# Weight splits and layer 0's state space tables on GpSimd in a two-layer hybrid decoder step

## The chip, the cores and the metric

The kernel runs on one core of one Trainium2 chip. The metric is the device time of one execution in microseconds, as the median of several runs.

## What is computed

One inference step of a decoder trunk with two layers, for one prompt of 512 tokens and eight samples of 4 tokens each (544 columns together), model width 1024, all in float32. Each layer, cut to what matters:

```
mod  = silu(c) @ w_ada + b_ada                  # 6 x 1024 values for each sequence
h    = rms_norm(x) * (1 + scale1) + shift1
proj = h @ w_in                                 # 1024 -> 1536: q, k, v, u, xr, yg
o    = concat(norm(window_attention(q, k, v)),  # 8 heads, 2 kv heads, window 128
              norm(s5_mixer(u)),                # 16 groups, complex state of 64
              norm(rglru_mixer(xr, yg)))        # depthwise conv, gated recurrence
x    = x + gate1 * (o @ w_o)
h2   = rms_norm(x) * (1 + scale2) + shift2
x    = x + gate2 * conv_ffn(h2)                 # 1024 -> 5632 -> conv 3 -> gelu gate -> 1024
```

The outputs are x and the new caches and states. The s5 mixer is a diagonal complex recurrence; its step a_bar = exp(lambda dt) and the factors in front of B come from the parameters alone, so that their powers and products can be put into tables before the tokens are there.

## The kernel before

**Matrix products.** Tokens lie along the free axis, in two halves of 256 and 288 columns. Each float32 product is made of three fp32r products: the weight is split into a rounded high part and a low part, `lo = raw - hi`, the activations likewise into `hh` and `hl`, and `mm3` (L430) adds hi x hh, hi x hl and lo x hh in PSUM. A weight tile (128 x 8 x 128) takes 48 such matmuls for both halves.

**Weights.** `Weights.ahead` (L407 to L417) loads the next weight of a fixed order into one of three `raw` buffers (L412, on the DMA queue of SyncE, SP), ScalarE rounds it to `whi` (L415), VectorE subtracts `wlo = raw - whi` (L416). There are six pairs of `whi` and `wlo`. Each time a weight has been used up, `done` frees its pair and calls `ahead` for one more. So the next six weights are split ahead of use. The `raw` buffers are shared with the slabs of the modulation weights `wada` (L507), of 512 KB each, which TensorE multiplies directly (L524); a `raw` buffer is free again when its slab has been multiplied, or its weight been split.

**Stages.** A start (the first slabs, the first norm, three weights), then for each layer the mixers and the feed-forward. In the mixers 12 column blocks of `w_in` are multiplied one after the other; each one's result starts a chain (attention, state space, recurrence) written as a generator, and after each product `tick` lets every chain take a step, lets attention do a unit, and lets the background do one slab of modulation weights. The 8 blocks of `w_o` follow as soon as all parts of `o` are there. In the feed-forward 44 blocks of `w_up` and three passes of 8 blocks of `w_down` follow each other, and layer 1's tables are made in the background. Tile, the framework, takes the order of the calls as priorities and settles each engine's order when the program is built; on the chip each engine and each DMA queue works its list strictly in order.

**Tables of the state space part.** `ssm_rot` (L759) makes the rotations `er`, `ei` for both halves of the groups in four stages, each by a complex product `cmul` (L577): four products, a difference, a sum. `ssm_tables` (L682) makes, for each half h, three complex products of 64, 192 and 256 elements per partition, widens them on ScalarE, multiplies them on TensorE into a direct kernel `kk`, clears a tile (L741), and spreads `kk` over it through a scratch tensor in DRAM (L744, L746). All tables are written to DRAM by DMAs on GpSimd's queue (`emit_tab`, L670) and read back on SP's queue (`load_tabs`, L678) by `ssm_chain`. In layer 0 this is called at the start of the mixers, between the first group of products, and the second half's tables go on as one of the chains. The tiles come from an arena of free tiles; `ssm_chain` waits for eight of them, so it follows the tables of the other half.

**GpSimd** does nothing else now than clear the `kz` tiles (L1459) and start DMAs: the tables above and the outputs.

Of the kernel before, what the change touches and what calls it, by code (L numbers as in the profile page):

```python
# [316 lines left out]
def trunk(ctx: ExitStack, tc: tile.TileContext, A, O):  # L317
    nc = tc.nc
    V, S, T_, G = nc.vector, nc.scalar, nc.tensor, nc.gpsimd
# [6 lines left out]
    def const(name, shape, dt=F32, pool=cp):  # L326
        return pool.tile(list(shape), dt, name=name)
# [59 lines left out]
    def f32(ap):  # L387
        return ap.bitcast(F32)
# [8 lines left out]
    class Weights:  # L397


        def __init__(self, order):  # L400
            self.order = list(order)
            self.free = [(const(f"whi{i}", (128, 8, 128), F32R), const(f"wlo{i}", (128, 8, 128), F32R))
                         for i in range(NW)]
            self.at = {}
            self.slot = {}

        def ahead(self, n=NW):  # L407
            while self.order and self.free and n:
                n -= 1
                key, src, kt = self.order.pop(0)  # L410
                raw = wp.tile([128, 8, 128], F32, tag="raw", name="raw", bufs=NRAW)[:, :kt]
                nc.sync.dma_start(raw, src)  # L412
                self.slot[key] = self.free.pop(0)
                hi, lo = (z[:, :kt] for z in self.slot[key])
                S.copy(hi, raw)  # L415
                V.tensor_sub(lo, raw, f32(hi))  # L416
                self.at[key] = (hi, lo)  # L417

        def __getitem__(self, key):
# [154 lines left out]
        ts(ki, k, 127.0, 8388608.0, OP.add, OP.mult)  # L574
        stt(out, pl, 1.0, ki.bitcast(F32), OP.add, OP.mult)

    def cmul(ore, oim, ar, ai, br, bi, t):  # L577
        V.tensor_mul(t, ai, bi)
        V.tensor_mul(ore, ar, br)
        V.tensor_sub(ore, ore, t)  # L580
        V.tensor_mul(t, ai, br)
        V.tensor_mul(oim, ar, bi)
        V.tensor_add(oim, oim, t)

    def ssm_params(l):
        d = LY[l]
# [77 lines left out]
    def bc(ap, w):  # L664
        return ap[:, :, None].to_broadcast([128, 4, w])
# [16 lines left out]
    def ssm_tables(l, h):  # L682
        d = LY[l]
        pw, kap = d["pw"], d["kap"]
        q = slice(4 * h, 4 * h + 4)
        yield from slots(7)
        raw, tm_, Z = R(512), R(512), R(512)
        nc.sync.dma_start(raw[:, 0:256].rearrange("p (a b) -> p a b", a=4),
                          A["ssmw"][l, :, :, q, :].rearrange("p a j c -> p a (j c)"))
        nc.sync.dma_start(raw[:, 256:512].rearrange("p (a b) -> p a b", a=2),  # L690
                          A["ssmc"][l, :, :, q, :].rearrange("p a j c -> p a (j c)"))
        rw = raw[:, 0:256].rearrange("p (a j c) -> p a j c", a=4, j=4)
        c0r = raw[:, 256:384].rearrange("p (j c) -> p j c", j=4)
        tm = tm_[:, 0:256].rearrange("p (j a c) -> p j a c", j=4, a=4)
        C0i = tm_[:, 256:384].rearrange("p (j c) -> p j c", j=4)
        Zr, Zi = (Z[:, 256 * i:256 * i + 256].rearrange("p (j s c) -> p j s c", j=4, s=4) for i in range(2))

        def bcn(ap, n):
            return ap[:, q, :, None].to_broadcast([128, 4, n, 16])

        def many(ap, n):
            return ap[:, :, None, :].to_broadcast([128, 4, n, 16])

        def widen(z, sign):

            o = R(512)
            ov = o.rearrange("p (j s g c) -> p j s g c", j=4, s=4, g=2)
            for g in range(2):
                act(ov[:, :, :, g], z, AF.Copy, scale=gm[:, sign + g:sign + g + 1])
            return o  # L710

        yield 1
        cmul(Zr[:, :, 3], Zi[:, :, 3], bc(kap[0][:, q], 16), bc(kap[1][:, q], 16), rw[:, 0], rw[:, 1], tm[:, :, 0])
        cmul(Zr[:, :, 0:3], Zi[:, :, 0:3], bcn(d["pwd"][0], 3), bcn(d["pwd"][1], 3),
             many(Zr[:, :, 3], 3), many(Zi[:, :, 3], 3), tm[:, :, 0:3])
        Br, Bi = widen(Zr, 0), widen(Zi, 0)
        Brv, Biv = (z.rearrange("p (j s c) -> p j s c", j=4, s=4) for z in (Br, Bi))
        yield 1
        ts(C0i, raw[:, 384:512].rearrange("p (j c) -> p j c", j=4), -1.0)
        cmul(Zr, Zi, bcn(d["pwu"][0], 4), bcn(d["pwu"][1], 4), many(rw[:, 2], 4), many(rw[:, 3], 4), tm)  # L720
        Cr, Ci = widen(Zr, 0), widen(Zi, 2)
        Crv, Civ = (z.rearrange("p (j d c) -> p j d c", j=4, d=4) for z in (Cr, Ci))
        yield 1
        pk = one()
        for part, (bb, c0, cc) in enumerate(((Brv, c0r, Crv), (Biv, C0i, Civ))):
            for jj in range(4):
                rows = slice(32 * jj, 32 * jj + 32)
                T_.matmul(pk[rows, 0:32], bb[:, jj, 3, :], c0[:, jj, :], start=part == 0, stop=part == 1,
                          skip_group_check=True)
            for jj in range(4):  # L730
                rows = slice(32 * jj, 32 * jj + 32)
                T_.matmul(pk[rows, 32:128], bb[:, jj, 3, :],
                          cc[:, jj, 0:3].rearrange("p d c -> p (d c)"), start=False, stop=part == 1,
                          skip_group_check=True)
        kk = sp.tile([128, 128], F32, tag="kk", name="kk", bufs=1)
        S.copy(kk, pk[:, :128])
        PS.put(pk)
        dg = d["prm"]("ssmd")[:, 32 * h:32 * h + 32]
        V.tensor_add(kk[:, 0:32], kk[:, 0:32], dg)
        tz = Z  # L740
        V.memset(tz, 0.0)  # L741
        tzv = tz.rearrange("p (j t) -> p j t", j=4)
        scr = tc.dram_tile([4, 32, 128], F32, name=f"kscr{l}{h}")
        G.dma_start(scr.rearrange("j c t -> (j c) t"), kk)  # L744
        for s in range(4):
            G.dma_start(tzv[32 * s:32 * s + 32, :, 32 * s:128],  # L746
                        scr[:, :, 0:128 - 32 * s].rearrange("j c t -> c j t"))
        emit_tab(l, h, "tz", tz)
        emit_tab(l, h, "cr", Cr)
        emit_tab(l, h, "ci", Ci)  # L750
        for n, z, o in (("br", Br, raw), ("bi", Bi, tm_)):
            yield 1
            ps = one()
            for jj in range(4):
                T_.transpose(ps[:, jj * 128:jj * 128 + 128], z[:, jj * 128:jj * 128 + 128], eye)
            S.copy(o, ps)
            PS.put(ps)
            free(z)
            emit_tab(l, h, n, o)  # L759
        d["ready", h] = True  # L760

    def ssm_rot(l):
        d = LY[l]
        E = []
        for h in range(2):
            er, ei = T(512), T(512)
            er, ei = (z.rearrange("p (j k) -> p j k", j=4) for z in (er, ei))
            V.memset(er[:, :, 0:1], 1.0)
            V.memset(ei[:, :, 0:1], 0.0)
            E.append((er, ei))  # L770
        tm = T(512)
        for st in range(4):
            m, n = (1, 1) if st == 0 else (2 * 4 ** (st - 1), 3)
            for h in range(2):
                er, ei = E[h]
                q = slice(4 * h, 4 * h + 4)

                def grid(z, lo, k):
                    return z[:, :, lo:lo + k * m].rearrange("p j (r k) -> p j r k", k=m)

                def factor(i):
                    return d["pow3"][i][:, st, q, 0:n, None].to_broadcast([128, 4, n, m])

                def base(z):
                    return z[:, :, None, 0:m].to_broadcast([128, 4, n, m])

                tv = tm[:, :4 * n * m].rearrange("p (j r k) -> p j r k", j=4, r=n)
                cmul(grid(er, m, n), grid(ei, m, n), factor(0), factor(1), base(er), base(ei), tv)
            yield
        free(tm)  # L790
        for h in range(2):
            emit_tab(l, h, "er", E[h][0].rearrange("p j k -> p (j k)"))
            emit_tab(l, h, "ei", E[h][1].rearrange("p j k -> p (j k)"))
# [942 lines left out]
    free(sg_)  # L1736
    W_ = Weights(weights_order())
    for l in range(L):
        with tc.tile_pool(name=f"mix{l}", bufs=1, reuse_waits="tile") as pool, ExitStack() as stack:
            banks(f"mb{l}", stack, 0, 4)  # L1740
            assert AR.kept == 0
# [43 lines left out]
            mixers(l, pool)  # L1785
            AR.free = [t for t in AR.free if any(t is p for p in perm)]
            assert len(AR.free) == NF, len(AR.free)
        with tc.tile_pool(name=f"ffn{l}", bufs=1, reuse_waits="tile") as pool, ExitStack() as stack:
            banks(f"fb{l}", stack, 1, 2)
            if l + 1 < L:  # L1790
                bg.append(tables(l + 1))
            ffn(l, pool)
            flush()
# [18 lines left out]
```

## Time and profile before

| what | value |
|---|---|
| median of 3 runs | 1328.41 us (1324.43 to 1328.97) |
| profiled execution | 1335.0 us |
| its span, first to last instruction | 1333.2 us |
| TensorE busy | 1270.1 us, 95% |
| VectorE busy | 881.8 us, 66% |
| ScalarE busy | 576.5 us, 43% |
| GpSimd busy | 48.8 us, 4% |

Busy times are those of engine instructions; waiting, branching and the issuing of DMAs on SP's and ScalarE's queues do not count here, while GpSimd's own DMA instructions do. PE is TensorE, PEld its weight loads, DVE VectorE, ACT ScalarE, POOL GpSimd. A time in the rows is counted from the first instruction of the span. Layer 0's mixers run from the start to about 295 us, layer 1's from about 700 to 930 us; the feed-forward parts lie behind each.

### The profile page before, as it was taken

How to read it: one execution, taken by the hardware profiler on the slowest of the kernel's cores; microseconds unless marked ns; L12 is line 12 of the kernel's file. 1: busy time of each engine (PE TensorE's matmuls, PEld its weight loads, DVE VectorE, ACT ScalarE, POOL GpSimd, SP SyncE). 2: the span in 40 equal slices, each digit the busy share in tenths (PEclk: the TensorE clock that was granted, in tenths of full speed). 3: DMA queues.
4: the chain of work that ended last, by engine and by line, in shares of the span. 5: the costliest groups of instructions: out<-in, count | busy, mean ns of one | idle time of the engine just before them, and what ended most of it. 6: DMA issues, size and time to landing. Idle time of an engine off the chain costs nothing.

```text
span 1333.2 us, 26368 instructions
## 1 busy us (share of the span) xinstructions
PE 1270.1 (95%) x10438; PEld 1164.8 (87%) x10438; DVE 881.8 (66%) x2583; ACT 576.5 (43%) x1112; POOL 48.8 (4%) x82
## 2 busy tenths in 40 slices
PE   4899988999999999999999999899999999999998
PEld 2666765799999999999998776679999999999998
DVE  8787885988774556456576877668865456545651
ACT  4557544356542343234354466545643234313430
POOL 0021010000020000000000001000000000000000
PEclk9899999999999999999999999999999999999999
DMA  8876677533343223334235846602322332233221
GB/s 294 279 265 215 191 252 229 178 111 118 93 135 125 85 86 87 97 93 115 76 108 180 268 142 203 191 14 90 110 81 86 96 95 74 86 97 94 85 72 51
DMA packets 72460, 178.24 MB, mean 134 GB/s; under 512 B 15584, under 2 KB 26752, under 8 KB 72336
## 3 DMA queue, kind: packets, MB, share of 16 engines
q1 hardware_dynamic: 65456, 162.08, 39.1%
q0 software_dynamic: 4960, 11.68, 2.5%
q10 hardware_dynamic: 1920, 2.79, 0.7%
q8 instruction: 82, 1.34, 0.4%
q14 instruction: 42, 0.34, 0.1%
HBM read 159.37 MB, written 14.34 MB: 130 GB/s over the span
## 4 chain that ended last, share of the span: by engine, by line
PE 83%; DMA 9%; DVE 5%; ACT 2%; issue 1%; POOL 0%; SPq 0%; DVEq 0%; POOLq 0%; ACTq 0%
PE wide L430 42%; PE fb1w L430 9%; PE fb0w L430 8%; DMA raw<-in_wada_dram 6%; PE fb0s L430 5%; PE fb1s L430 4%; PE mb0s L430 3%; PE mb1s L430 3%; PE mb0s L524 1%; PE mb1s L524 1%; DMA raw<-in_wo_dram 1%; DVE wlo L416 1%; DMA f<-in_ssmh_dram 1%; DMA tab_br<-f 1%; PE mb1s L1242 0%
## 5 line engine op out<-in xcount | busy, mean ns | idle before, releaser
L430 PE MATMUL wide<-hh,whi 128*128 128x288 f32 (+1 forms) x1360 | 400.3, 295 | 1.2 <-ACT hh L897 0.8
L430 PE MATMUL wide<-hl,whi 128*128 128x288 f32 (+1 forms) x1360 | 395.9, 291 | 0.0
L430 PE MATMUL wide<-hh,wlo 128*128 128x288 f32 (+1 forms) x1360 | 394.3, 290 | 0.0
L416 DVE TENSOR_TENSOR wlo<-raw,whi 128x1024 fp32r<-128x1024 f32 (+1 forms) x176 | 211.0, 1200 | 187.1 <-ACT whi L415 183.1
L415 ACT CAST whi<-raw 128x1024 fp32r<-128x1024 f32 (+1 forms) x176 | 180.4, 1029 | 274.8 <-PE wide L430 125.8
L430 PEld LDWEIGHTS wide<-hh,whi 128*128 128x128 f32 x1360 | 257.2, 189 | 18.3 <-issue 14.0
L430 PEld LDWEIGHTS wide<-hl,whi 128*128 128x128 f32 x1360 | 257.1, 189 | 6.3 <-issue 6.1
L430 PEld LDWEIGHTS wide<-hh,wlo 128*128 128x128 f32 x1360 | 259.2, 191 | 3.0 <-issue 3.0
L380 DVE SCALAR_TENSOR_TENSOR f<-wide,prm,f 128x511 f32<-128x511 f32 x236 | 100.2, 485 | 0.0
L430 PE MATMUL wide<-mid,whi 128*128 128x256 f32 (+1 forms) x526 | 99.8, 287 | 0.0
L430 PEld LDWEIGHTS wide<-mid,whi 128*128 128x128 f32 x526 | 82.4, 188 | 0.0
L897 ACT CAST mid<-f 128x544 fp32r<-128x544 f32 x44 | 28.5, 647 | 122.4 <-DVE f L1660 119.1
L430 PE MATMUL wide<-mid,wlo 128*128 128x256 f32 (+1 forms) x263 | 75.5, 287 | 0.0
L377 ACT ACTIVATE f<-f 128x544 f32<-128x544 f32 x50 | 33.0, 659 | 89.2 <-DVE f L1650 84.5
L430 PE MATMUL fb1w<-hh,whi 128*128 128x256 f32 (+1 forms) x240 | 69.4, 289 | 1.8 <-ACT hh L862 1.3
L430 PE MATMUL fb1w<-hl,whi 128*128 128x256 f32 (+1 forms) x240 | 69.4, 289 | 0.0
L430 PE MATMUL fb1w<-hh,wlo 128*128 128x256 f32 (+1 forms) x240 | 68.8, 287 | 0.0
L430 PE MATMUL fb0w<-hh,whi 128*128 128x256 f32 (+1 forms) x224 | 64.7, 289 | 1.6 <-ACT hh L862 1.1
L430 PE MATMUL fb0w<-hl,whi 128*128 128x256 f32 (+1 forms) x224 | 64.7, 289 | 0.0
L430 PE MATMUL fb0w<-hh,wlo 128*128 128x256 f32 (+1 forms) x224 | 64.3, 287 | 0.0
L430 PE MATMUL fb0s<-mid,whi 128*128 128x288 f32 (+1 forms) x326 | 62.9, 290 | 0.0
L430 PE MATMUL fb1s<-mid,whi 128*128 128x288 f32 (+1 forms) x308 | 59.1, 289 | 0.0
(612 smaller groups left out, 2542.2 us busy)
## 6 DMA issues: line engine op xcount, KB each, us to landing
raw<-in_wada_dram SPq DMA_DIRECT2D x92, 512.0 KB, 5.2
raw<-in_wup_dram SPq DMA_DIRECT2D x88, 512.0 KB, 3.5
raw<-in_wdn_dram SPq DMA_DIRECT2D x32, 448.0 KB, 3.3
raw<-in_win_dram SPq DMA_DIRECT2D x24, 512.0 KB, 4.2
raw<-in_wo_dram SPq DMA_DIRECT2D x16, 512.0 KB, 4.5
raw<-in_wdn_dram SPq DMA_DIRECT2D x16, 512.0 KB, 3.5
e<-q ACTq DMA_DIRECT2D x32, 68.0 KB, 4.6
out_ox_dram<-x SPq DMA_DIRECT2D x8, 272.0 KB, 2.1
```

Source lines behind the costliest of these rows:

```text
L377: return S.activation(out, in_, f, bias=bias, scale=scale, **kw)
L380: return V.scalar_tensor_tensor(out, a, s, b, op0=op0, op1=op1, **kw)
L415: S.copy(hi, raw)
L416: V.tensor_sub(lo, raw, f32(hi))
L430: T_.matmul(out, w[wi][:, k, :], r[ri][:, a:b], start=first and i == 0, stop=last and i == 2)
L524: T_.matmul(ps[32 * g:32 * g + 32], silu[:, k, :], have[n][:, g], start=k == 0, stop=k == 7, skip_group_check=True)
L897: S.copy(dst[0], src)
```

## The change

In `Weights` the engine of the subtraction becomes a variable, which is GpSimd at the start and in the mixers, and VectorE in the feed-forward. `cmul` takes an engine; in `ssm_tables` and `ssm_rot` this is GpSimd for layer 0 and VectorE for layer 1, and so is the engine that clears the tile before the direct kernel is spread. The memsets at the start of `ssm_rot` and the sign change `C0i` stay on VectorE.

```
@@ Weights
+            self.low = G
...
                 S.copy(hi, raw)
-                V.tensor_sub(lo, raw, f32(hi))
+                self.low.tensor_sub(lo, raw, f32(hi))
@@ cmul
-    def cmul(ore, oim, ar, ai, br, bi, t):
-        V.tensor_mul(t, ai, bi)
-        V.tensor_mul(ore, ar, br)
-        V.tensor_sub(ore, ore, t)
-        V.tensor_mul(t, ai, br)
-        V.tensor_mul(oim, ar, bi)
-        V.tensor_add(oim, oim, t)
+    def cmul(ore, oim, ar, ai, br, bi, t, eng=None):
+        z = eng or V
+        z.tensor_mul(t, ai, bi)
+        z.tensor_mul(ore, ar, br)
+        z.tensor_sub(ore, ore, t)
+        z.tensor_mul(t, ai, br)
+        z.tensor_mul(oim, ar, bi)
+        z.tensor_add(oim, oim, t)
@@ ssm_tables
+        eng = V if l else G
...
-             many(Zr[:, :, 3], 3), many(Zi[:, :, 3], 3), tm[:, :, 0:3])
+             many(Zr[:, :, 3], 3), many(Zi[:, :, 3], 3), tm[:, :, 0:3], eng)
...
-        V.memset(tz, 0.0)
+        eng.memset(tz, 0.0)
@@ ssm_rot
-                cmul(grid(er, m, n), grid(ei, m, n), factor(0), factor(1), base(er), base(ei), tv)
+                cmul(grid(er, m, n), grid(ei, m, n), factor(0), factor(1), base(er), base(ei), tv, V if l else G)
@@ main loop
     for l in range(L):
+        W_.low = G
...
             mixers(l, pool)
...
+        W_.low = V
         with tc.tile_pool(name=f"ffn{l}", bufs=1, reuse_waits="tile") as pool, ExitStack() as stack:
```

The other two calls of `cmul` in `ssm_tables` take `eng` in the same way.

## Rows read from the trace of the kernel before

**Rows 1.** The page: busy us (share of the span) and instructions of each engine.
```profile
PE 1270.1 (95%) x10438; PEld 1164.8 (87%) x10438; DVE 881.8 (66%) x2583; ACT 576.5 (43%) x1112; POOL 48.8 (4%) x82
```

**Rows 2.** The page: the chain that ended last, share of the span by engine.
```profile
PE 83%; DMA 9%; DVE 5%; ACT 2%; issue 1%; POOL 0%; SPq 0%; DVEq 0%; POOLq 0%; ACTq 0%
```

**Rows 3.** Windows: us, PE, PEld, DVE, ACT, POOL busy (x), PEclk, DMA share, GB/s.
```profile
0.00:320.00 320.00, 278.10 (x2381) 214.65 (x2382) 257.74 (x1046) 170.12 (x379) 26.21 (x46) 0.97 0.67 216
690.00:950.00 260.00, 243.24 (x2026) 202.48 (x2025) 199.03 (x657) 147.22 (x325) 10.51 (x14) 0.99 0.49 151
...
990.00:1023.00 33.00, 33.00 (x266) 33.00 (x265) 18.78 (x38) 13.90 (x23) 0.00 (x0) 1.00 0.28 82
```

**Rows 4.** Waits of PE, 28 to 320 us: us in total, times, longest us.
```profile
PE mb0s L524 <- DMA raw<-in_wada_dram: 11.0, 9, 2.4
PE mb0s L430 <- ACT hh L862: 4.2, 1, 4.2
PE mb0s L1263 <- DVE pm L384: 3.8, 3, 1.5
...
PE mb0s L430 <- DVE hl L863: 1.3, 2, 0.8
...
PE mb0s L459 <- DVE half L1126: 1.1, 2, 0.8
```

**Rows 5.** Waits of PE, 690 to 950 us.
```profile
PE mb1s L524 <- DMA raw<-in_wada_dram: 9.3, 10, 1.7
PE mb1s L430 <- ACT hh L862: 1.4, 1, 1.4
PE fb1w L430 <- ACT hh L862: 1.3, 1, 1.3
```

**Rows 6.** Timeline of DVE: start us, us, instruction (count) [idle before <-releaser].
```profile
25.52 1.22 DVE L416 TENSOR_TENSOR wlo<-raw,whi 128x1024 fp32r<-128x1024 f32 x1
...
27.47 1.22 DVE L416 TENSOR_TENSOR wlo<-raw,whi 128x1024 fp32r<-128x1024 f32 x1
28.60 0.42 DVE L863 TENSOR_TENSOR hl<-half,hh 128x256 fp32r<-128x256 f32 x1
...
111.32 1.22 DVE L416 TENSOR_TENSOR wlo<-raw,whi 128x1024 fp32r<-128x1024 f32 x1
```

**Rows 7.** Windows of single lines (L578, then L583): us, DVE busy (x), PEclk, DMA.
```profile
17.00:38.00 21.00, 2.30 (x8) 1.00 0.93 321
...
17.00:38.00 21.00, 2.36 (x9) 1.00 0.93 321
61.00:75.00 14.00, 1.58 (x5) 1.00 0.81 266
100.00:103.00 3.00, 0.42 (x1) 1.00 0.61 172
```

**Rows 8.** Groups of POOL, 0 to 320 us: count | busy us, mean ns | idle before.
```profile
L746 POOL DMA_DIRECT2D f<-kscr x8 | 4.4, 558 | 6.9 <-PE wide L430 5.1 <-DVE wlo L416 1.8
...
L670 POOL DMA_DIRECT2D tab_tz<-f x2 | 1.1, 559 | 9.2 <-DMA f<-kscr 9.2
...
L1459 POOL MEMSET kz<- 64x512 f32 x2 | 1.0, 518 | 0.3 <-POOLq L1801 0.3
...
L1801 POOL MEMSET const-float32-1.0<- 128x1 f32 x1 | 0.1, 109 | 0.0
```

**Rows 9.** Timeline of PE, the first products.
```profile
27.50 0.58 PE L430 MATMUL mb0s<-hh,whi 128*128 128x256 f32 x1 [4.21 <-ACT hh L862]
...
29.08 0.58 PE L430 MATMUL mb0s<-hl,whi 128*128 128x256 f32 x1 [0.78 <-DVE hl L863]
```

**Rows 10.** Timeline of ACT, one cast of a weight.
```profile
106.22 1.05 ACT L415 CAST whi<-raw 128x1024 fp32r<-128x1024 f32 x1 [0.87 <-PE wide L430]
```

**Rows 11.** Waits of SP's DMA queue, 28 to 320 us: us in total, times, longest.
```profile
SPq L507 <- DVE wlo L416: 7.7, 5, 2.0
```

**Rows 12.** The chain that ended last, 60 to 200 us: start us, us, what.
```profile
114.90 6.94 DMA tab_br<-f
```

More of the change, by code (lines that the diff above doesn't have):

```diff
@@ L712, in ssm_tables @@
         yield 1
-        cmul(Zr[:, :, 3], Zi[:, :, 3], bc(kap[0][:, q], 16), bc(kap[1][:, q], 16), rw[:, 0], rw[:, 1], tm[:, :, 0])
+        cmul(Zr[:, :, 3], Zi[:, :, 3], bc(kap[0][:, q], 16), bc(kap[1][:, q], 16), rw[:, 0], rw[:, 1], tm[:, :, 0], eng)
         cmul(Zr[:, :, 0:3], Zi[:, :, 0:3], bcn(d["pwd"][0], 3), bcn(d["pwd"][1], 3),
-             many(Zr[:, :, 3], 3), many(Zi[:, :, 3], 3), tm[:, :, 0:3])
+             many(Zr[:, :, 3], 3), many(Zi[:, :, 3], 3), tm[:, :, 0:3], eng)
         Br, Bi = widen(Zr, 0), widen(Zi, 0)
@@ L719, in ssm_tables @@
         ts(C0i, raw[:, 384:512].rearrange("p (j c) -> p j c", j=4), -1.0)
-        cmul(Zr, Zi, bcn(d["pwu"][0], 4), bcn(d["pwu"][1], 4), many(rw[:, 2], 4), many(rw[:, 3], 4), tm)
+        cmul(Zr, Zi, bcn(d["pwu"][0], 4), bcn(d["pwu"][1], 4), many(rw[:, 2], 4), many(rw[:, 3], 4), tm, eng)
         Cr, Ci = widen(Zr, 0), widen(Zi, 2)
```

## The prediction

> **What bounds the kernel now.** I read the engine summary first [rows 1]: TensorE is busy for 1270.1 of 1333.2 us, VectorE for 66%, GpSimd for 4%. So nothing that frees VectorE is worth more than the time in which TensorE stands still, 63 us in all. The chain that ended last says the same: 83% of it is TensorE, 9% DMA, 5% VectorE [rows 2]. Then I cut the span by stage [rows 3]. In the feed-forward parts, where the change leaves everything as it is, TensorE is busy for all of 33.00 us while VectorE has 14 us to spare. In the two mixers (with the turn to the feed-forward: 0 to 320 us and 690 to 950 us) TensorE is idle for 320.00 - 278.10 = 41.9 us and 260.00 - 243.24 = 16.8 us, and there VectorE is busy for 257.74 and 199.03 us, 81% and 77%. These 58.7 us are the whole stake. The waits of TensorE say who ended them [rows 4, 5]: the largest share is 11.0 and 9.3 us of matmuls on the modulation weights that wait for their DMA into a `raw` buffer. VectorE, or ScalarE work that stands behind VectorE's, ended less: in layer 0 4.2 us before the first projection matmul, then 3.8, 1.3 and 1.1 us and others no longer than that; in layer 1 1.4 and 1.3 us and shorter ones.
>
> **What VectorE is rid of.** The slots of the weights settle which low parts move: 3 and then 3 more before layer 0's mixers, and one for each of the 20 weights that are used up in a mixer part. That is 26 in layer 0 and 20 in layer 1 (layer 1's first six are subtracted in the feed-forward, still on VectorE). At 1.22 us each [rows 6] this is 46 x 1.22 = 56 us. The complex products of layer 0's tables fill lines 578 to 583: in 17 to 38 us the six rows are 2.30 to 2.36 us from the first to the last line, 13.9 us together; in 61 to 75 us six of some 1.6, 9.9 us; in 100 to 103 us five of 0.42, 2.1 us [rows 7]. With two memsets of 0.5 us (estimated at GpSimd's own price for 512 elements [rows 8]) VectorE loses 27 + 56 = 83 of the 457 us that it is busy in the mixers, 27 + 32 = 59 of them in layer 0.
>
> **What GpSimd gets.** No row shows GpSimd subtracting. What it shows is a memset of 512 elements in 0.52 us and one of a single element in 0.11 us [rows 8], so 0.1 us fixed and 0.82 ns for each element of one stream. A subtraction reads two streams and writes one. The lower bound is one stream's time, 0.1 + 1024 x 0.82 ns = 0.94 us, the upper three streams in turn, 0.1 + 3 x 0.84 = 2.6 us. I take 2.2 us, near the upper end: GpSimd needs for writing alone 0.82 ns an element, where VectorE needs 1.2 ns for the whole subtraction. The page "GPSIMD Engine Reference" of the Trainium skill (section 3.1) gives 4497 ns for a two-input add of 2048 elements, half of which is an estimate of 2.25 us; the sum below would be the same by it. The 84 products and sums of the tables have 12,240 elements in all: between 18 and 39 us of GpSimd, 33 at the middle pace, against 26 us on VectorE. In layer 0 GpSimd then has 26 x 2.2 + 33 = 90 us of new work beside 26 us of old [rows 3]: it has room.
>
> **Step by step on the path.**
> (a) Start. VectorE's list at 25 to 30 us [rows 6] has three low parts of 1.22 us, and table products, in front of and between the low parts `hl` of the activations. The first `hl` began at 28.60, right behind a weight; its high part had released TensorE's first product at 27.50, and the next but one then waited 0.78 us for `hl` [rows 9]. I take 28.60 - 27.50 = 1.1 us gained. Bounds: 2.4 us gained, if both weights ahead of it held it; 4.1 us lost, if at GpSimd's upper price the third of three weights in a row comes 3 x (2.6 - 1.22) us later and TensorE stands for all of it.
> (b) Layer 0 behind the start: the waits that VectorE ended are 3.8 + 1.3 + 1.1 us and, in the same view, shorter ones of about 2 us, some 8 us [rows 4]. VectorE loses 59 of 258 us, a quarter of its work, and it is an in-order queue that is 81% full, so its delays shrink by more than that quarter; I take half, 4 us (bounds 0 and 8).
> (c) The `raw` buffers. Three serve the weights and the modulation slabs, and a weight's is free again when its low part is done. On VectorE a low part starts late where the queue is long: that of the cast that ended at 107.27 started at 111.32 [rows 6, 10]. Over the 46 pairs this wait is 0.03 to 4.7 us, 36.9 us together, 0.8 us on average, and seven pairs over 2 us hold 22.8 of it. On GpSimd the buffer is free 2.2 us after the cast, on VectorE 0.8 + 1.22 = 2.0: nothing on average, but the seven late ones come 2.3 us earlier each, and the DMA queue SP stood behind a low part in front of slab loads in 5 places of layer 0 [rows 11]. I take 2 us off the 20.3 us of slab waits (bounds: 4 lost, 6 gained).
> (d) Layer 1 loses 24 of 199 us of VectorE. Its waits are 1.4 + 1.3 us and about 3 us of shorter ones [rows 5]; I take a third, 2 us (bounds 0 and 5).
> (e) GpSimd's queue. A low part can now stand behind GpSimd's own DMA waits: in layer 0's two tables it waits 6.9 us and 9.2 us for the scratch round trip [rows 8]. One or two weights can be caught, and five others stand ready ahead of each; I charge 1 us. The rotation tables, which VectorE has done by 38 us [rows 7], are read only with the state tables, whose last DMA stands in the chain at 114.90 us [rows 12]: there a slower engine costs nothing. On that last DMA's way are the five products at 100 to 103 us. They come out even, at 0.42 us now against about 0.6 (0.1 + 256 x 2.05 ns), but without a weight of 1.22 us among them.
> Sum: -1.1 - 4 - 2 - 2 + 1 = -8.1 us. The profiled execution took 1335.0 us, 1333.2 in its span and 1.8 around it, and would take 1326.9; it is 6.6 us above the median of the runs, 1328.4, from which the sum gives 1320.3. I say **1320 us**. Its own range is 1310 to 1326.
>
> **Rivals.**
> 1. Hidden anyway. TensorE's own order and the slab loads keep the ends where they are, and (b) to (d) shrink to 1 or 2 us: 1325 to 1330 us. For it: the slab waits are the largest row in both mixers [rows 4, 5], and the longest wait for `hl` in all of layer 0 is under 1 us [rows 4]. Against it: late low parts reach the slabs through the `raw` buffers.
> 2. The two engines get in each other's way. The low parts read two tiles of SBUF, and so do `half`, `hl` and most of VectorE's list. If VectorE has to stand still while GpSimd subtracts, each low part costs VectorE 2.2 us in place of 1.22. Three of them fall into each of the start and the two turns to the feed-forward, where TensorE has nothing else: 3 x 3 x (2.2 - 1.22) = 8.8 us lost, and no relief elsewhere: 1337 us. It decides as soon as GpSimd holds VectorE for longer than 1.22 us a time. No row here can speak on it, as GpSimd reads no tile with an engine instruction now. The page "SBUF — State Buffer" of the Trainium skill (section "Who interferes with whom") states just this: a VectorE instruction with two SBUF inputs and a GpSimd instruction that reads SBUF exclude each other for a whole instruction. By that rule the time would be this rival's; I give it no more than its chance because much of VectorE's list in the mixers has PSUM or one tile as input, and because in a gap of VectorE's the low part costs nothing.
> 3. GpSimd's queue becomes the wait. It waits for four round trips of 2 to 6 us in layer 0 [rows 8], and some four weights' low parts can fall behind them. If each holds its `raw` buffer 4 us longer and the slab behind it is late by 2.5 us, 10 us are lost against half of the relief, 4: 1334 us.
>
> **How the numbers follow.** A measurement of this kernel tells about 0.5% (6.6 us) from no change. Forecast 0.46: 0.40 of it beyond 0.5%, 0.06 within. Hidden 0.28: 0.04 faster, 0.21 within, 0.03 slower. Engines in each other's way 0.14: 0.03 within, 0.11 slower. Queue 0.12: 0.02 within, 0.10 slower. Together: faster 0.44, same 0.32, slower 0.24. The low end takes the gains at their bounds without the whole of (c): 2.4 + 8 + 5 + 4 = 19, so 1309; the high end is rival 2's 1337.
>
> **What would show it.** GpSimd's low parts at 2 to 2.6 us, 46 of them; VectorE at 60 to 65% in the mixers with lists that no longer wait; TensorE's waits for `pm`, `hl` and `half` halved; slab waits a little under 20 us; feed-forward unchanged. I am wrong if VectorE's instructions with two SBUF tiles get longer or start late beside GpSimd's (rival 2), if SP waits for a low part for several us beside a GpSimd DMA wait (rival 3), or if the mixers end where they did.

## The result, and the profile after

The changed kernel took **1396.85 us** (median of 4 runs, 1393.08 to 1401.19) against 1327.16 us for the kernel before on the same chip (1324.43 to 1328.97): a ratio of **1.0528** [1.0485, 1.0571], 5% slower where 1320 us was forecast. The profiled execution has a span of 1398.0 us against 1333.2.

The page of the kernel after, engine summary and chain that ended last, answers to [rows 1] and [rows 2]:

```profile
PE 1286.9 (92%) x10438; PEld 1181.4 (85%) x10438; DVE 913.1 (65%) x2451; ACT 582.2 (42%) x1116; POOL 204.2 (15%) x214
...
PE 76%; DVE 11%; DMA 5%; POOL 4%; issue 2%; ACT 2%; SPq 0%; ACTq 0%; DVEq 0%; POOLq 0%
```

VectorE runs 132 instructions fewer (46 low parts, 84 products and sums, 2 memsets), and is busy 31 us **more**. That is the line to stop at: an engine that lost work can only be busier if what is left became longer. In the chain VectorE has gone from 5% to 11%, GpSimd from nothing to 4%.

The windows of the kernel after, cut at the same points of the work (layer 0 with the turn to the feed-forward, layer 1 with the turn, a stretch of feed-forward), in the columns of [rows 3]:

```profile
0.00:361.70 361.70, 285.53 (x2381) 222.59 (x2382) 281.83 (x934) 175.78 (x383) 130.05 (x158) 0.94 0.60 191
731.70:1014.90 283.20, 252.68 (x2026) 211.22 (x2025) 206.36 (x637) 147.32 (x325) 62.08 (x34) 0.95 0.45 139
1054.90:1087.90 33.00, 33.00 (x265) 33.00 (x265) 18.79 (x38) 13.91 (x23) 0.00 (x0) 1.00 0.26 81
```

The feed-forward of layer 0, first before, then after:

```profile
320.00:690.00 370.00, 370.00 (x3012) 369.14 (x3011) 219.06 (x467) 136.54 (x222) 11.48 (x21) 1.00 0.33 100
```

```profile
361.70:731.70 370.00, 370.00 (x3012) 369.15 (x3011) 218.95 (x467) 136.48 (x222) 11.50 (x21) 1.00 0.32 100
```

Layer 0 takes 361.7 us in place of 320, layer 1 283.2 in place of 260; the feed-forward, where nothing is changed, takes what it took. 41.7 + 23.2 = 64.9 us is the whole loss. Of it TensorE stands still for 34.3 us more in layer 0 (76.2 against 41.9) and 13.7 us more in layer 1 (30.5 against 16.8); the other 16.9 us are matmuls that took longer, in mixers whose granted clock is 0.94 and 0.95 of full speed on the mean, 0.97 and 0.99 before. I read the lower clock as following from TensorE's new waits; no run tests that.

The waits of TensorE in layer 0 (28 to 361.7 us) answer to [rows 4]:

```profile
PE mb0s L431 <- POOL wlo L417: 13.6, 1, 13.6
PE mb0s L934 <- ACT e L377: 10.0, 1, 10.0
PE mb0s L1245 <- DVE q L1225: 6.4, 3, 2.5
PE mb0s L525 <- DMA raw<-in_wada_dram: 5.3, 7, 1.9
PE fb0s L460 <- DVE sqacc L840: 3.3, 1, 3.3
...
PE wide L479 <- DVE qr L380: 2.4, 2, 2.1
PE mb0s L479 <- DVE qr L380: 2.4, 1, 2.4
```

The first row is one wait, for the first low parts on GpSimd. The second is one for ScalarE; it was 0.4 us before. Then come waits for VectorE's `q`, `sqacc` and `qr`, of which no row over 0.7 us stood there before. (`e` holds the squares of a block of queries or keys for their norm, `sqacc` sums of squares; `qr`, `hr` and `rst` are steps of reciprocal roots on a few columns; `q` is a block of queries turned by its position tables.) The slab waits, the largest row before, are half of what they were.

Each kind is explained by a timeline. First GpSimd's, around the first low parts:

```profile
37.39 1.00 POOL L585 TENSOR_TENSOR g<-g,g 128x384 f32<-128x384 f32 x1
38.69 0.56 POOL L672 DMA_DIRECT2D tab_ei<-g x1 [0.30 <-POOL g L585]
39.27 6.97 POOL L417 TENSOR_TENSOR wlo<-raw,whi 128x1024 fp32r<-128x1024 f32 x3
```

GpSimd also takes its instructions in order, and all 48 rotation products (to 38.4 us) stand ahead of the first three low parts. The second, ScalarE's and then GpSimd's, ahead of the matmul that waits 10.0 us until 91.09:

```profile
89.62 0.51 ACT L377 ACTIVATE f<-f,gm 128x256 f32<-128x256 f32 x1 [3.53 <-POOL f L585]
...
90.43 0.60 ACT L377 ACTIVATE e<-wide 128x544 f32<-128x544 f32 x1
```

```profile
85.23 0.63 POOL L583 TENSOR_TENSOR f<-pwu,g 128x256 f32<-128x256 f32 x1
85.82 2.38 POOL L417 TENSOR_TENSOR wlo<-raw,whi 128x1024 fp32r<-128x1024 f32 x1
88.17 0.62 POOL L584 TENSOR_TENSOR f<-pwu,g 128x256 f32<-128x256 f32 x1
88.86 0.72 POOL L585 TENSOR_TENSOR f<-f,f 128x256 f32<-128x256 f32 x1
```

ScalarE widens the state tables' products (`f<-f,gm`), and its list is in order too: TensorE's `e` stands behind a product that now comes from GpSimd, and there behind a low part. Then VectorE's timeline, at the start and at four later places:

```profile
31.74 15.38 DVE L840 TENSOR_TENSOR sqacc<-sqacc,half 128x288 f32<-128x288 f32 x7
...
62.02 2.55 DVE L859 TENSOR_TENSOR half<-x,sqacc 128x256 f32<-128x256 f32 x1
...
111.14 2.35 DVE L445 TENSOR_TENSOR rst<-hr 128x40 f32<-128x40 f32 x1
...
129.69 2.37 DVE L385 TENSOR_SCALAR hr<-rst 128x40 int32<-128x40 int32 x1
...
315.97 2.30 DVE L385 TENSOR_SCALAR qr<-rst 128x2 int32<-128x2 int32 x1
```

An operation on 40 elements takes 2.35 us, one on 2 elements 2.30. Beside the last three, GpSimd's timeline has:

```profile
110.58 2.86 POOL L417 TENSOR_TENSOR wlo<-raw,whi 128x1024 fp32r<-128x1024 f32 x1 [0.35 <-ACT whi L416]
...
129.47 2.54 POOL L417 TENSOR_TENSOR wlo<-raw,whi 128x1024 fp32r<-128x1024 f32 x1 [0.57 <-ACT whi L416]
...
315.86 2.39 POOL L417 TENSOR_TENSOR wlo<-raw,whi 128x1024 fp32r<-128x1024 f32 x1 [3.62 <-ACT whi L416]
```

Each of these three VectorE instructions begins after a low part has begun and ends 0.02 to 0.05 us after it: 111.14 + 2.35 = 113.49 against 110.58 + 2.86 = 113.44. That is a hold, not slow work. The groups of VectorE with one shape each show how large it is in all, first before, then after:

```profile
L837 DVE TENSOR_TENSOR sqacc<-sqacc,half 128x288 f32<-128x288 f32 x28 | 12.7, 453 | 1.0 <-ACT half L377 1.0
L908 DVE TENSOR_TENSOR x<-x,rs 128x32 f32<-128x32 f32 x64 | 12.2, 190 | 1.5
...
L385 DVE TENSOR_SCALAR qr<-rst 128x2 int32<-128x2 int32 x6 | 1.0, 168 | 0.1
```

```profile
L840 DVE TENSOR_TENSOR sqacc<-sqacc,half 128x288 f32<-128x288 f32 x28 | 34.9, 1246 | 4.9 <-ACT half L377 4.3
L911 DVE TENSOR_TENSOR x<-x,rs 128x32 f32<-128x32 f32 x64 | 20.1, 314 | 1.6
...
L385 DVE TENSOR_SCALAR qr<-rst 128x2 int32<-128x2 int32 x6 | 5.3, 876 | 0.1
```

Over all VectorE instructions of unchanged count, each shape against its own mean before, this comes to 93 us.

### The profile page after: what moved, and what is told of

Its sections match the earlier page's. It is cut to its first block, busy times and chain, and to the rows that moved or that the text cites. A ratio compares the mean times of both kernels' runs of the same rounds, so it can differ in the third digit from the quotient of the medians.

```text
span 1398.0 us, 26388 instructions
## 1 busy us (share of the span) xinstructions
PE 1286.9 (92%) x10438; PEld 1181.4 (85%) x10438; DVE 913.1 (65%) x2451; ACT 582.2 (42%) x1116; POOL 204.2 (15%) x214
## 4 chain that ended last, share of the span: by engine, by line
PE 76%; DVE 11%; DMA 5%; POOL 4%; issue 2%; ACT 2%; SPq 0%; ACTq 0%; DVEq 0%; POOLq 0%
PE wide L431 38%; PE fb1w L431 8%; PE fb0w L431 7%; PE fb0s L431 4%; PE fb1s L431 4%; DMA raw<-in_wada_dram 4%; PE mb0s L431 2%; PE mb1s L431 2%; POOL wlo L417 1%; PE mb0s L525 1%; PE mb0s L1245 1%; PE mb1s L525 1%; DVE sqacc L840 1%; DVE half L859 1%; DVE f L1060 1%
## 5 line engine op out<-in xcount | busy, mean ns | idle before, releaser
L431 PE MATMUL wide<-hh,whi 128*128 128x288 f32 (+1 forms) x1360 | 405.2, 299 | 1.6 <-ACT hh L900 0.8
L431 PE MATMUL wide<-hh,wlo 128*128 128x288 f32 (+1 forms) x1360 | 398.4, 293 | 1.5 <-POOL wlo L417 1.5
L431 PEld LDWEIGHTS wide<-hh,whi 128*128 128x128 f32 x1360 | 260.8, 192 | 18.4 <-issue 14.1
L417 DVE TENSOR_TENSOR wlo<-raw,whi 128x1024 fp32r<-128x1024 f32 (+1 forms) x130 | 154.9, 1192 | 174.3 <-ACT whi L416 170.6
L431 PEld LDWEIGHTS wide<-hl,whi 128*128 128x128 f32 x1360 | 261.0, 192 | 7.0 <-issue 6.3
L431 PEld LDWEIGHTS wide<-hh,wlo 128*128 128x128 f32 x1360 | 262.9, 193 | 4.5 <-issue 2.6
L417 POOL TENSOR_TENSOR wlo<-raw,whi 128x1024 fp32r<-128x1024 f32 x46 | 116.2, 2534 | 248.8 <-ACT whi L416 241.3
```

What stands on the lines that cost most here:

```text
L417: self.low.tensor_sub(lo, raw, f32(hi))
L431: T_.matmul(out, w[wi][:, k, :], r[ri][:, a:b], start=first and i == 0, stop=last and i == 2)
```

## The experiments

Three theories were open. A *hold* is the time for which one engine's instruction keeps another engine's from going on. **P**: a GpSimd instruction that reads SBUF holds VectorE's instructions for its length. **Q**: GpSimd's own queue brings the low parts too late. **W** (from the fifth run on): what costs time is that casts and low parts must wait for GpSimd at all. Times below are medians; the ratio to the kernel before on the same chip has its 95% interval.

**Tables alone, low parts alone.** Each is the changed kernel with the other part back on VectorE: the first edit keeps the low parts there, the second the tables (the argument in `ssm_rot` changes in the same way and is left out here).

```diff
-        W_.low = G
+        W_.low = V
```

```diff
-        eng = V if l else G
+        eng = V
```

> The tables of layer 0 on GpSimd, all low parts of the weights on VectorE as before. Theory P (ports: while GpSimd reads SBUF, a VectorE instruction with two SBUF inputs stands still): the 84 short GpSimd instructions of 0.2 to 1.1 us hold VectorE in the first 110 us, 3 to 12 us slower than before. Theory Q (queue order: the loss comes from low parts that stand behind other work on GpSimd and are long in coming): no low part is on GpSimd, so within 3 us of before or a little faster.

> The 46 low parts on GpSimd, the tables on VectorE as before; on GpSimd's list the first three low parts now come at once, not behind the rotation products. Theory P: layer 1's mixers lose their 23 us as in the changed kernel, layer 0's somewhat more, 35 to 50 us slower than before. Theory Q: with nothing in front of the low parts the loss of the start (some 15 us and what follows from it) goes, and what is left is 46 low parts of 2.4 in place of 1.2 us, 0 to 15 us slower than before.

Tables alone: 1340.91 us, 1.0059 [1.0039, 1.008], about 8 us lost, where P had 3 to 12. Low parts alone: 1383.54 us, 1.0374 [1.0346, 1.0402], 50 us lost, the upper end of P's range and far above Q's 15. So neither part gains, and the low parts make most of the loss. Together they make 4.3%, and the change 5.3%. With the tables alone TensorE's wait for ScalarE's `e` is there already, 6.2 us (with the low parts alone it is 4.0):

```profile
PE mb0s L934 <- ACT e L377: 6.2, 1, 6.2
```

**The queue at the start.** VectorE does the first three low parts, all else as in the change.

```diff
-        W_.low = G
+        W_.low = G if l else V
...
                         W_.ahead(GRP)
+                        W_.low = G
```

> The changed kernel, but the first three low parts (before the first product) on VectorE. Theory P and Q agree that TensorE's wait of 13.6 us for the first low part goes. P: 45 to 55 us slower than before remain. Q: 15 to 35 us remain, as the start was the larger part of layer 0's loss.

1390.23 us, 1.044 [1.0403, 1.0477]. The 13.6 us wait is gone, and 0.9% (about 12 us) of the 5.3% with it: what is left, 4.4%, is the two parts' own losses added (4.3%), a little more than P's 45 to 55 us and far more than Q's 35. Queue order is real, and about a sixth of the loss.

**Work that nobody wants.** In the kernel before, GpSimd makes an unused subtraction at 40 places, in the low part just freed; VectorE then overwrites it. In this run and its partners `self.low` only says that the mixers are being built.

```diff
+                if self.low and len(self.order) < self.total - NW:
+                    G.tensor_sub(lo, f32(hi), f32(hi))
                 S.copy(hi, raw)
                 V.tensor_sub(lo, raw, f32(hi))
```

> The kernel before, and in the mixers a further subtraction on GpSimd for each weight that is fetched into a used pair (20 a layer): hi - hi of the old pair into the freed low part, before the new one is cast; its result is written over and nobody's input hangs on it but the next cast of that pair. Theory P: 40 instructions of 2.4 us that read SBUF hold VectorE, 15 to 35 us slower than before, and VectorE instructions of 0.2 us appear with 2 us and more. Theory Q: GpSimd's results are wanted by nobody, so within 5 us of before.

1378.26 us, 1.0343 [1.0312, 1.0373]. VectorE still does all its work and gets nothing late from GpSimd, yet 46 us are lost, more than the 15 to 35 that P had: a loss of this size needs no result of GpSimd's. But the waits of ScalarE showed a second way in this run, 39.0 us in 18 waits of casts for the unused subtraction, since it reads the high part that the cast overwrites. So its partner fills both parts and reads nothing:

```diff
-                    G.tensor_sub(lo, f32(hi), f32(hi))
+                    G.memset(f32(hi), 0.0)
+                    G.memset(f32(lo), 0.0)
```

> The kernel before, with 40 unused GpSimd writes: where the run with unused subtractions reads the old high part, this one fills the freed high and low part with zeros (two memsets of 1024 elements, about 0.94 us each, so about 1.9 us as in that run), ahead of the new cast. The new cast and VectorE's subtraction wait for GpSimd exactly as they did there; but GpSimd reads nothing. Theory P (GpSimd's reading of SBUF holds VectorE): VectorE's instructions keep their durations, and the time is that of the kernel before plus what the casts lose by waiting 1.9 us for a fill, 1330 to 1345 us, well under the 1378 of the run with subtractions. Rival W (the unused subtractions cost their 46 us because the casts and low parts had to wait for them in GpSimd's queue): 1370 to 1385 us again. The two are told apart at 1357.

1347.80 us, 1.0126 [1.0109, 1.0142]: a little over P's bound, far below W's. And one that reads a single stream, in the same place:

```diff
+                    G.tensor_copy(lo, f32(hi))
```

> The same 40 unused GpSimd instructions as a copy of the old high part into the low part: one stream read in place of two, then overwritten by VectorE. The casts and low parts wait as in the run with subtractions. Theory P in its plain form (any GpSimd instruction that reads SBUF holds VectorE for its whole length): the added time scales with the length of the copy; at 1.0 to 1.9 us a copy, 1350 to 1378 us, with VectorE's instructions stretched. Theory P2 (only GpSimd's two-input instructions hold VectorE): near the run with memsets, 1330 to 1345 us, VectorE's durations as before. Rival W: as the memsets, whatever those give.

1353.91 us, 1.0178 [1.0156, 1.0199], inside P's range and above P2's 1345. The casts wait as long for the copies (23.8 us) as for the two memsets (22.9 + 1.4 us), and still 0.5% more is lost. Two timelines of this run, VectorE's and GpSimd's, speak against P2, the idea that only two-input instructions of GpSimd hold:

```profile
292.63 1.61 DVE L860 TENSOR_TENSOR half<-x,sqacc 128x256 f32<-128x256 f32 x2
```

```profile
292.93 1.04 POOL L418 CAST wlo<-whi 128x1024 fp32r<-128x1024 f32 x1 [3.22 <-PE mb0s L434]
```

Two instructions that take 0.75 us where nothing holds them (last rows of the next pair) take 1.61 beside one copy. So a copy holds as well; it is only 1.05 us long (median). How much of this run's loss is hold was not taken apart.

**The hold alone.** The cleanest pair takes the casts' wait away. GpSimd subtracts two constant tiles, or fills the low part twice; both times only VectorE's own low part comes behind it.

```diff
+                    G.tensor_sub(lo, eye[:, None, :].to_broadcast([128, kt, 128]), ones[:, None, :].to_broadcast([128, kt, 128]))
```

```diff
+                    G.memset(f32(lo), 0.0)
+                    G.memset(f32(lo), 0.0)
```

> The kernel before with the same 40 unused GpSimd subtractions, but of two constant tiles (the identity less the ones, each read eight times over, 1024 elements), written to the freed low part. No cast waits for GpSimd any more; only VectorE's own low part, which overwrites the result, does. What is left of the 46 us is then the hold alone. Theory P: the run with memsets showed 17 us for the waits and left some 30 for the hold, so 1355 to 1370 us, and VectorE's instructions with one or two SBUF tiles as input stretch by about 2 us where they meet one. Rival W (what cost the time was the casts' wait on GpSimd): within 6 us of the run that only fills the low part.

> Its partner: two memsets of 1024 elements on the freed low part at each of the 40 places (1.9 us), no cast waits for GpSimd, nothing is read. Theory P: two-input instructions of VectorE run as before; only its one-input instructions (scalings by constants, copies) that meet a memset are held, up to 1 us each: 1330 to 1343 us. Rival W: the run with memsets on both parts lost 17 us through the casts' waits, so this one loses 5 at most, and the run with constants no more than this one.

With reading 1391.12 us, 1.0427 [1.0397, 1.0458]; without 1339.50 us, 1.0059 [1.0037, 1.0081]. VectorE waits equally long for either (6.8 and 6.7 us in all), so **the 52 us between them are the hold and what follows from it**: 40 subtractions, 97.0 us of GpSimd in all, of which about half reached the end. VectorE is busy for 950.0 us in place of 885.3 with the same 2583 instructions. TensorE is busy for 1290.9 us in place of 1273.1, at a mean granted clock of 0.974 in place of 0.990: some 18 of the 54 us between the profiled executions (1389.0 and 1335.0 us) are slower matmuls, the rest are waits. P had expected 1355 to 1370; part of the miss is that subtracting two tiles takes 2.39 us (median) and a tile from itself only 1.89, the rest stays open. W falls. The same VectorE instruction beside a subtraction and beside a memset, in the first run VectorE's and GpSimd's timeline:

```profile
973.83 2.96 DVE L860 TENSOR_TENSOR half<-x,sqacc 128x256 f32<-128x256 f32 x2
```

```profile
974.09 2.41 POOL L418 TENSOR_TENSOR wlo<-eye,ones 128x1024 fp32r<-128x1024 f32 x1 [0.81 <-PE mb1s L434]
```

and in the second, VectorE's (two places) and GpSimd's:

```profile
280.73 0.88 DVE L385 TENSOR_SCALAR qr<-rst 128x2 int32<-128x2 int32 x1
...
926.12 0.75 DVE L861 TENSOR_TENSOR half<-x,sqacc 128x256 f32<-128x256 f32 x2
926.79 0.75 DVE L868 TENSOR_TENSOR hl<-half,hh 128x256 fp32r<-128x256 f32 x2
```

```profile
280.61 0.97 POOL L419 MEMSET wlo<- 128x1024 f32 x1
...
926.44 0.95 POOL L418 MEMSET wlo<- 128x1024 f32 x1 [1.23 <-PE mb1s L435]
```

Beside a memset the two-input pairs take 0.75 us each, beside a subtraction 2.96. But the memset does hold the first row, an instruction with one input and 2 elements: 0.88 us, to 0.03 us after the memset's end. Such holds are part of the 8 us or so that the memsets cost.

**Shorter holds.** Each of the 43 low parts that GpSimd has when VectorE does the first three is cut into four pieces.

```diff
-                self.low.tensor_sub(lo, raw, f32(hi))
+                for p in range(0, kt, 2 if self.low is G else kt):
+                    q = slice(p, p + (2 if self.low is G else kt))
+                    self.low.tensor_sub(lo[:, q], raw[:, q], f32(hi[:, q]))
```

> The run in which VectorE does the first three low parts (1390 us), with each of GpSimd's 43 low parts cut into four pieces of 256 elements (about 0.65 us each, some 2.6 us together). Theory P with holds that end with each GpSimd instruction: VectorE gets in between two pieces, so an instruction of a short chain waits for at most one piece, 0.6 us in place of 2.3; the stretch of VectorE's instructions (88 us in that run) falls by a third or more and the time to 1355 to 1380 us. Rival L (what counts is how long GpSimd works beside VectorE in all, not how long one hold is, or GpSimd takes the port again at once): 1385 to 1400 us.

1383.71 us, 1.0401 [1.038, 1.0422], not told apart from 1.044 with whole low parts; it lies between P's 1380 and L's 1385 us. P's form with gaps was too hopeful: the stretch of VectorE fell from 88 to 75 us, since a piece takes 0.74 us (median) and four take 2.96 where one low part takes 2.39. Shorter holds brought little here, where GpSimd read for longer in all; the two effects were not taken apart.

**Layer 1 alone.** The 20 low parts of layer 1 on GpSimd, everything in layer 0 on VectorE.

```diff
-        W_.low = G
+        W_.low = G if l else V
```

> The change in layer 1 alone: 20 low parts on GpSimd, layer 0 with its tables as in the kernel before. GpSimd's list there is short (no table products, DMA issues only), so theory Q (GpSimd's queue) has little to say: 0 to 5 us lost. Theory P: in the run with all 46 low parts the casts of layer 1 fell behind by a further 20 us, and the first layer hands nothing on but a shift: 1348 to 1355 us. The prediction's own step had 2 us gained.

1350.58 us, 1.013 [1.01, 1.0159]: 18 us lost, as P had it, with no table product on GpSimd. TensorE's waits in that layer (685.4 to 961.1 us): behind two for DMAs (9.3 and 1.3 us before) come waits for the same short instructions as in layer 0:

```profile
PE mb1s L525 <- DMA raw<-in_wada_dram: 6.0, 7, 1.2
PE mb1s L1084 <- DMA f<-tab_ci: 5.6, 1, 5.6
PE fb1s L460 <- DVE sqacc L840: 3.0, 1, 3.0
PE mb1s L1245 <- DVE q L1225: 2.2, 1, 2.2
PE wide L479 <- DVE qr L380: 2.1, 1, 2.1
```

## Why the prediction was wrong

**The step that failed is the weight and the size given to rival 2.** It named the mechanism (the engines in each other's way) and its turning point, a hold of over 1.22 us, but charged it only at the start and the two turns, "3 x 3 x (2.2 - 1.22) = 8.8 us lost, and no relief elsewhere", and gave it 0.14. The holds measure 2.1 to 2.2 us beyond an instruction's own length, and they cost time all through the mixers: the low parts alone lost 50 us, and 40 subtractions that nobody needs 52 more than memsets. Both reasons for the small chance fell. "Much of VectorE's list in the mixers has PSUM or one tile as input" goes against the rival's own opening, where most of that list reads two tiles, and one-input instructions on a few elements were held as well (`qr` and `hr` above). "In a gap of VectorE's the low part costs nothing": a queue that is 77 to 81% full has few, and a hold that falls on `rst`, `qr`, `q` or `sqacc` falls on a chain of small dependent steps with TensorE at its end. The page "SBUF — State Buffer" of the Trainium skill (section "Who interferes with whom") says that a two-input VectorE instruction excludes a GpSimd one that reads, and that copies and operations of a tile with scalars can contend with GpSimd too, for a whole instruction. The traces agree on both counts: 2.96 us beside a subtraction against 0.75 beside a memset for the first, 0.88 us beside a memset for the second. No row of the trace before could price it, as the prediction said; but with all 46 places in it the rival's own sum would have been 46 x (2.2 - 1.22) = 45 us, where the low parts alone measured 50. That the two lie so close is partly luck: about half of the unused subtractions' time reached the end, so 46 of them would cost some 46/40 x 52 = 60 us (an estimate), and taking 56 us off VectorE gave back about 10.

**(a) Start**: 1.1 us gained was forecast, 4.1 lost at the worst; the wait is 13.6 us, and taking it away returned about 12. The step asked how long three low parts take on GpSimd and not what stands ahead of them there. The prediction itself moved the 48 rotation products to that queue, and only asked when their tables are read.

**(b) and (d)**, the relief of VectorE: 4 and 2 us gained were forecast. Its work did leave (132 instructions), but the rest grew by more, and the new waits for VectorE in layer 0 are for that rest. With layer 1 changed alone, 18 us were lost in place of 2 gained.

**(c) Raw buffers**: the slab waits did shrink (11.0 to 5.3 us in the row of layer 0), though SP's queue waits for low parts for longer ahead of slabs, 40.2 us in layer 0 in place of 7.7. TensorE's waits for slabs are no part of the loss.

**(e)** and rival 3 looked for GpSimd's delay behind its DMA waits; it came from its own products. "Read only with the state tables" was said of the rotation tables; that ScalarE's list stands behind the products of the state tables at 61 to 75 us was not asked, and is the 6.2 us of the tables alone. Rival 1 (hidden anyway) falls with the verdict.

**Right** were the prices on GpSimd: 2.39 us a low part (median; 2.2 taken, 2.6 the bound), and 204.2 - 48.8 - 116.2 = 39 us for the tables (33 taken, 39 the bound); and that the feed-forward stays as it was. The sum was wrong because those prices were weighed against GpSimd's idle time, and a large part of them is VectorE's time as well.

## What to carry to other kernels

Before moving elementwise work from VectorE to GpSimd, count the GpSimd instruction's whole length as time in which VectorE's SBUF work may stand still; instructions that only write cost far less here (80 memsets, some 8 us). Compare that length with what VectorE is rid of: here a low part was up to 2.39 us of hold against 1.22 us of relief, and it lost. And list the target engine's own queue in order, and who waits for each result: what is moved first delays what is moved next. The runs point to no split of this work that beats the kernel before, so none was tried.

## What was not expected of the hardware

- The hold works both ways. The source view of GpSimd's low parts after the change (min/median/max in ns):

```profile
L417 POOL TENSOR_TENSOR wlo<-raw,whi x46: 2338/2390/5484, 39.3 to 994.2; 128x1024 fp32r<-128x1024 f32 x46
```

  One of them took 5.48 us, from 780.57 to 786.05. In that time VectorE ran two-input products without a gap until 783.81, and the low part ended 2.24 us after the last of them.
- GpSimd's price goes by what it reads: for 1024 elements a memset took 0.95 us, a copy 1.05, a subtraction of a tile from itself 1.89, one of two tiles 2.39.
- At the start seven `sqacc` steps of 0.45 us took 15.38 us together, in a stretch in which GpSimd ran one product after the other and then three low parts: without gaps between its instructions, VectorE got in about once in 2 us.
